# Three queues re-ordered in a gated conv/attention block on one Trainium2 core: weight sums, the first down chunk, and the last products

## The chip, the core and the metric

The kernel runs on one core of a Trainium2 chip. The metric is the device time of one execution in microseconds (us), taken as the median of several. A second source is one profiled execution, whose rows carry a start time, a duration, the engine and a line number (L326 is line 326). PE is TensorE, PEld its weight loads, DVE VectorE, ACT ScalarE, POOL GpSimd, SP SyncE; SPq, POOLq and ACTq rows are DMAs issued by those engines.

## What is computed

The reference is one layer of a streaming encoder over 512 positions and 1024 channels, in float32:

```
h = rms_norm(x)
[conv B | conv C | conv in | q | k | v | forget | gates] = h @ w_in
y_A = (B * dwconv3(C * xin)) @ w_out_conv ;  y_B = forgetting_attention(q, k, v) @ w_out_attn
x = x + (sigmoid(g_A) * y_A + sigmoid(g_B) * y_B) @ w_o
[a | b] = dwconv3(rms_norm(x) @ w_up)
x = x + (silu(a) * b) @ w_down
out = rms_norm(x)
```

`w_up` has 2 x 2816 columns, which are 44 blocks of 128, called up0 to up43 (block 2j is a, block 2j+1 is b of pair j, and j runs from 0 to 21). `w_down` has 2816 rows.

## The kernel before, in words

**Three products for one.** Activations stand transposed: 128 partitions of channels, 512 columns of positions. Each float32 factor is split into a high part in a shorter format and the rest (`hi`, `lo`), and a product is three TensorE passes, wh*xh, wl*xh and wh*xl (`mm3`, L300, and `passes`, L314). So each chunk of weights that is loaded is also split (`split`, L252): ScalarE copies it to `wh` (L274), VectorE subtracts to get `wl` (L278). Both have two buffers, so a chunk can be split while the one before it is in use. `passes` takes all products with wh first and those with wl after them, so `wl` may come later than `wh`. A whole up block takes TensorE 5.44 us; its first two of eight row blocks go through `passes`, which uses wl after eight matmuls.

**Seven products for eight.** Part of the gates (j from 3 to 7), up pairs 1, 2 and 5 (`SUP`), and most of the down projection are computed in pairs of 2x2 blocks with seven block products (`seven`, L786). Their weights come in two chunks for each step, P (plain blocks) and F (sums of blocks). The sums are made by DMAs between DRAM tensors `f` (`make_forms`, L190): six operations for each group of steps, alternately a copy issued by SP (`put`) and an adding DMA issued by POOL (`add`): f0 = x0, f0 += x1, f1 = f0, f1 += x1, f2 = f1, f2 += x2. Each waits for the one before it to land. They stand in a list with a slot number, and each call of `slot()` (L217) issues those that are due.

**The gate loop** (L947 to L979) runs over eight output blocks j. In each: `slot()` (L949), the two gate blocks, then the chunk mix j, then two products yc and ya with a `slot()` in front of each (L967), then the gating: two VectorE products (L975, L976), a POOL sum (L977), a ScalarE copy to `mh` (L978) and a VectorE subtraction to `ml` (L979). In j = 7 four loads of x are issued by POOL (L953) right after the first `slot()`. In this loop the list holds the sums for the up pairs 1, 2 and 5, three groups, with six operations each in slots 4k + g for operation k of group g: the copies f2 = f1 are in j = 5 (groups 0 and 1) and j = 6 (group 2), the last adds f2 += x2 are in j = 6 (group 0, third slot) and j = 7 (group 1 in the first slot, group 2 in the second).

**The order on an engine** is fixed before the launch by a planner: of the instructions that it reckons to be ready it takes the one that was written first. `keep` (L82) pins an instruction behind the one that was written just before it on the same engine, whatever that is. The DMAs of `slot()`, the loads of chunks and all matmuls are pinned. L953 and L977 are not.

**Evacuations put off.** `later` is a list of pieces of work with a price in us and a chunk from which they are due. `run_later` (L223), called by each `split`, issues pieces from the front of the list up to a budget (0.1 more is allowed), behind the two instructions of that split. Pieces that merge the seven-product up pairs (`merge`, L1150) carry a mark "e": z1 0.42, m1 0.7, u3 0.85, m2 0.7, fin0 0.7, tap0 1.4, fin1 0.7, tap1 1.4, and `glu`. While a marked piece is in the list, the budget is that of L285 (3.8 for an up chunk), and each further up block's evacuation is put on the list too, with the mark: a product with the norm factor (`mul`, 0.7, L1139), the causal filter (`taps`, 1.4: one ScalarE copy and two VectorE instructions, L561 to L565) and after the second block `glu`. Without a marked piece an evacuation is written at once, and the budget is 1.7 (L287). `glu` (L1195) multiplies silu(a) and b (POOL), and for each second pair adds six pieces that form and split the sums for the down projection (t13 and t24 at 0.85, four splits at 0.7; L1220 to L1233), due two to four chunks later, or four to six after the last pair of a phase, whose product goes to VectorE and is due three chunks later. If an older pair has such pieces left, `glu` first issues them all.

**Two phases.** Pairs 0 to 11 go through up and then the down projection (12 steps, P16 and F16 to P27 and F27), then pairs 12 to 21 and 8 steps (from P28). Between the up loop and the down projection all marked pieces are issued (L1311); `seven` then splits its first chunk unless that is done (`chunk`, L289). `split_next` (L780) splits the next chunk of the stream if it isn't split yet.

**The end.** The last two output blocks of the down projection are plain products in two halves of the columns; `fin_out` (L1376) then multiplies all eight blocks of a half with the norm factor, which TensorE has put into a PSUM bank `pb`, and stores them by five DMAs, from SP and ACT in turn. ScalarE copies the factor to `rs` in SBUF, since POOL does one of the five products and VectorE four.

Of the kernel before, what the change touches and what calls it, by code (L numbers as in the profile page):

```python
# [8 lines left out]
F32 = mybir.dt.float32  # L9
F32R = mybir.dt.float32r  # L10
AF = mybir.ActivationFunctionType
ALU = mybir.AluOpType

P = 128
D = 1024
S = 512
# [26 lines left out]
PHASES = ((0, 12), (12, NP))  # L43
# [27 lines left out]
def block_kernel(ctx, tc, xT, vecs, wv, win, wmix, wo, wup, wst, wdp, outT):  # L71
# [3 lines left out]
    nc = tc.nc  # L75
# [83 lines left out]
    def after_split():  # L159

        st = ExitStack()
        for ins in order.values():
            st.enter_context(tc.issue_after(ins))
        return st
# [4 lines left out]
    def load(upto):  # L169
        for k in range(len(raws), min(upto, len(stream) - 1) + 1):  # L170
            nm, src, ncol = stream[k]
            tag = tag_of(k)
            if held[tag] == NRAW[tag] or tag not in pools:
                return
            held[tag] += 1
            raw = pools[tag].tile([P, D], F32, tag=tag, name=f"raw_{nm}", bufs=NRAW[tag])
            if k == 0:

                keep(nc.scalar.dma_start(raw[:, VB:ncol], src[:, VB:]))
                keep(nc.sync.dma_start(raw[:, :VB], src[:, :VB]))  # L180
            else:
                keep(nc.sync.dma_start(raw[:, :ncol], src if tag == "raw" else made[src]))
            raws.append(raw[:, :ncol])
# [33 lines left out]
    def slot():  # L217

        while todo_bg and todo_bg[0][0] <= make_forms.slot:
            todo_bg.pop(0)[1]()  # L220
        make_forms.slot += 1

    def run_later(k, us):  # L223

        n = 0
        while n < len(later):
            if later[n][0] <= k and later[n][1] <= us + 0.1:
                us -= later[n][1]
                with after_split():
                    later.pop(n)[3]()  # L230
            elif later[n][0] <= k:
                return
            else:
                n += 1
# [17 lines left out]
    def split(hl=None):  # L252

        k = len(parts)
        if k == len(stream):
            return
        nm, _, ncol = stream[k]
        load(k + (LOOK if len(raws) > KB else AHEAD))
        if hl is None:
            hl = []  # L260
            for x in "hl":
                if k == 0:
                    wp.tile([P, PADW[x]], F32, tag=f"pad{x}", name=f"pad_{x}")
                w0 = VOFF if k < KB else 0
                hl.append(wp.tile([P, D], F32R, tag=f"w{x}", name=f"w{x}_{nm}", bufs=2)[:, w0 : w0 + ncol])
        hi, lo = hl
        raw = raws[k]
        if k == 0:
            for cs in (slice(VB, S + H), slice(0, VB)):
                keep(nc.vector.tensor_copy(hi[:, cs], raw[:, cs]))  # L270
        elif k == 1:
            keep(nc.vector.tensor_copy(hi, raw))
        else:
            ins = nc.scalar.activation(hi, raw, AF.Copy)  # L274
            order["hi"] = ins.ins
            if k < KB:
                keep(ins)
        ins = nc.vector.tensor_sub(lo, raw, hi.bitcast(F32))  # L278
        order["lo"] = ins.ins
        if k < KB:  # L280
            keep(ins)
        held[tag_of(k)] -= 1
        parts.append((hi, lo))
        if any(("e",) in w[2] for w in later):
            run_later(k, {"u": 3.8, "P": 1.6, "F": 1.2}[nm[0]])  # L285
            return
        run_later(k, {"u": 1.7, "P": 1.6, "F": 0.75, "i": 3.0, "m": 3.0, "d": 0 if nm == "dp1" else 2.1}.get(nm[0], 3.5))  # L287

# [123 lines left out]
    pb = [pb_[t // 2][:, (t % 2) * 4 * HD : (t % 2 + 1) * 4 * HD] for t in range(NT)]  # L412
# [333 lines left out]
    for idx in late:  # L746
        kind, i = divmod(idx, 4)
# [32 lines left out]
    def split_next():  # L780
        if len(parts) == chunk.n and stream[chunk.n][0] not in ("dp1", "dp2"):
            split()
# [104 lines left out]
    k = [c[0] for c in stream].index("mix1")  # L887
    for q in (0, 2):
        f, g = x_sums(slice(q, q + 2))
# [56 lines left out]
    make_forms(len(GATES), N0, "up")  # L946
    for j in range(KB):  # L947
        gs = []
        slot()  # L949
        if j == KB - 1:  # L950
            x1 = xp.tile([P, KB, S], F32, tag="x1", name="x1")
            for q in range(4):
                nc.gpsimd.dma_start(x1[:, 2 * q : 2 * q + 2, :], xT[:, 2 * q : 2 * q + 2, :])  # L953
        if j == 0:
            evac_gate(0, gs)(gp[0])
            evac_gate(8, gs)(gp[1])
        elif j < GJ:
            run_all(proj(20 + j, f"ga{j}", evac_gate(j, gs), acc))
            run_all(proj(28 + j, f"gb{j}", evac_gate(8 + j, gs), acc))
        else:  # L960
            if j == GJ:
                acc = ring(2, 7, 3, 4)
            seven(GATES[2 * (j - GJ) : 2 * (j - GJ) + 2], 2 * (j - GJ), {j: (0, 1, 5, 6)}, gate_form, done=gate_pair(j, gs))
        wh, wl = chunk(f"mix{j}")
        yc, ya = acc(f"yc{j}"), acc(f"ya{j}")
        for pp, hh, ll, o in ((yc, ych, ycl, 0), (ya, oth, otl, 4)):
            slot()  # L967
            for k in range(4):
                ks = slice((o + k) * P, (o + k + 1) * P)
                mm3(pp, wh[:, ks], wl[:, ks], hh[:, k, :], ll[:, k, :], k == 0, k == 3)  # L970
        if j >= GJ:
            split_next()
            flush()
        a, b = gs
        nc.vector.tensor_mul(a, a, yc)  # L975
        nc.vector.tensor_mul(b, b, ya)  # L976
        nc.gpsimd.tensor_add(a, a, b)  # L977
        nc.scalar.activation(mh[:, j, :], a, AF.Copy)  # L978
        nc.vector.tensor_sub(ml[:, j, :], a, mh.bitcast(F32)[:, j, :])  # L979
# [44 lines left out]
    def block(name, xh, xl, lead=False):  # L1024
        wh, wl = chunk(name)
        q = acc(f"p_{name}")
        for kb in range(KB):
            ks = slice(kb * P, (kb + 1) * P)
            if lead and kb < 2:
                if kb:  # L1030
                    passes([
                        (q[:, cs], 0, wh[:, b], wl[:, b], xh[:, a, cs], xl[:, a, cs], True, False)
                        for a, b in enumerate((slice(0, P), ks)) for cs in halves
                    ], 4)
                continue
            mm3(q, wh[:, ks], wl[:, ks], xh[:, kb, :], xl[:, kb, :], kb == 0, kb == KB - 1)
        return q
# [53 lines left out]
    fp = ctx.enter_context(tc.tile_pool(name="fp", bufs=1))  # L1091
# [22 lines left out]
    def up(j, ph, rb2, pu=None):  # L1114
        uu = []

        def tap(i, z):
            u = fp.tile([P, S], F32, tag="fu", name=f"fu{j}{i}", bufs=3)
            taps(u, z, CF + 3 * (2 * j + i))
            uu.append(u)  # L1120

        if j in SUP:
            c = len(GATES) + 2 * SUP.index(j)
            slot()
            seven(
                UPD[c - len(GATES) :][:2], c, {j: USETS[j]}, up_form, of="x",
                done=lambda i, banks, ids: merge(ph, j, banks, ids, rb2, tap, uu),
            )
            slot()
            return  # L1130
        evacs = []
        for i in range(2):
            slot()
            p = pu[i] if pu else block(f"up{2 * j + i}", x1h, x1l, True)
            z = [None]

            def mul(i=i, p=p, z=z):
                z[0] = fp.tile([P, S], F32, tag="fz", name=f"fz{j}{i}", bufs=4)
                nc.vector.tensor_mul(z[0], p, rb2)  # L1139

            evac = [(0.7, mul), (1.4, lambda i=i, z=z: tap(i, z[0]))]
            if i:
                evac.append((0, lambda: glu(ph, j, uu)))
            if any(("e",) in w[2] for w in later):
                later.extend((0, us, (("e",), acc.last) if x == 0 else (("e",),), f) for x, (us, f) in enumerate(evac))
            else:
                for _, f in evac:
                    f()
# [227 lines left out]
    def fin_out(t, rc):  # L1376
        hs = halves[t]
        pb = rstd_bc(rc, 2, (1, 5)[t], f"n3{t}")[:, : S // 2]
        rs = fp.tile([P, S], F32, tag="fu", name=f"rs{t}", bufs=3)[:, : S // 2]
        nc.scalar.activation(rs, pb, AF.Copy)  # L1380
        for g, (a, b) in enumerate(((0, 1), (1, 3), (6, 8), (3, 5), (5, 6))):
            y = x1[:, a:b, hs]
            eng, r = (nc.gpsimd, rs) if g == 2 else (nc.vector, pb)
            eng.tensor_mul(y, y, r.unsqueeze(1).to_broadcast([P, b - a, S // 2]))  # L1384
            keep((nc.sync, nc.scalar)[g % 2].dma_start(outT[:, a:b, hs], y))

    def warm_on(n):
# [121 lines left out]
```

## Time and profile before

| what | us |
|---|---|
| median of 3 runs (lowest to highest) | 697.87 (697.65 to 698.26) |
| the profiled execution, its own time | 698.61 |
| its span from first to last instruction | 696.8 |
| PE busy in the span | 686.7 |
| DVE, ACT, POOL busy | 530.9, 359.7, 180.7 |

The span is 1.8 us shorter than the time of its execution, and that execution is 0.74 us above the median. A row's bracket, as in "[1.55 <-ACT wh_P L274]", is the idle time of its engine just before it and the instruction that ended it. In a row with x6, six instructions in a row are merged. Matmuls overlap one another, so a matmul's duration (0.28 us) is longer than the step from one to the next (0.113 us).

### The profile page before, as it was taken

Reading aid. Unit: us, or ns where it says so; the run is one execution under the profiler, and the core shown is the slowest. Engines: PE = TensorE matmul, PEld = TensorE weight load, DVE = VectorE, ACT = ScalarE, POOL = GpSimd, SP = SyncE. Lnnn points to the kernel's source line nnn. Section 1 sums busy time; section 2 is a strip of 40 time slices with the busy share of each in tenths; the row PEclk is TensorE's granted clock in tenths of the full one; section 3 lists DMA queues with packets and bytes.
Section 4 is the critical chain, followed back from the end, with each engine's and each line's share of the span. In section 5 each row is a group of like instructions: output and inputs, shape, how many; then the busy total and the mean of one; then the engine's idle time right before and its main releaser. Section 6 shows DMA issues by size and latency. Waiting matters only on the chain.

```text
span 696.8 us, 14636 instructions
## 1 busy us (share of the span) xinstructions
PE 686.7 (99%) x5972; PEld 684.9 (98%) x5972; DVE 530.9 (76%) x824; ACT 359.7 (52%) x567; POOL 180.7 (26%) x196
## 2 busy tenths in 40 slices
PE   9999999999999999999999999999999999999996
PEld 9999999999999998999999999999999999999995
DVE  6677877776678776868869799988674677878793
ACT  5665655645565443446554455465443344445572
POOL 4134847532211201113523143210000313221001
PEclk9999999999999999999999999999999999999998
DMA  7528978542688687666799775536646686676513
GB/s 253 161 70 276 205 183 201 121 91 89 234 237 257 183 234 208 202 216 141 110 316 296 199 184 130 153 124 193 198 129 228 143 192 162 184 170 175 156 31 121
DMA packets 58387, 124.68 MB, mean 179 GB/s; under 512 B 5280, under 2 KB 26800, under 8 KB 58320
## 3 DMA queue, kind: packets, MB, share of 16 engines
q1 hardware_dynamic: 40776, 99.68, 44.0%
q0 software_dynamic: 16304, 22.88, 20.6%
q10 hardware_dynamic: 1240, 1.19, 0.5%
q8 instruction: 47, 0.77, 0.4%
q14 instruction: 20, 0.16, 0.1%
HBM read 121.57 MB, written 39.32 MB: 231 GB/s over the span
## 4 chain that ended last, share of the span: by engine, by line
PE 58%; DVE 2%; DMA 0%; ACT 0%; issue 0%; DVEq 0%; ACTq 0%
PE p_up L308 21%; PE dn L326 19%; PE p_up L326 7%; PE p_wo L308 6%; PE pdB L308 1%; PE pdA L308 1%; PE ya L308 1%; PE yc L308 1%; DMA raw_dp<-in_wdp_dram 0%; PE pc_n L343 0%; DVE fu L562 0%; DVE fu L565 0%; PE pb_n L362 0%; DVE gl L1231 0%; DVE wl_up L278 0%; DVE x L1384 0%
## 5 line engine op out<-in xcount | busy, mean ns | idle before, releaser
L308 PE MATMUL p_up<-x1h,wh_up 128*128 128x256 f32 x464 | 90.5, 276 | 0.0
L308 PE MATMUL p_up<-x1l,wh_up 128*128 128x256 f32 x464 | 90.3, 276 | 0.0
L308 PE MATMUL p_up<-x1h,wl_up 128*128 128x256 f32 x464 | 90.3, 276 | 0.0
L210 POOL DMA_DIRECT2D f<-in_wst_dram x57 | 66.1, 1311 | 15.6 <-DMA f<-f 15.3
L308 PEld LDWEIGHTS p_up<-x1h,wh_up 128*128 128x128 f32 x464 | 69.9, 188 | 0.0
L308 PEld LDWEIGHTS p_up<-x1l,wh_up 128*128 128x128 f32 x464 | 69.9, 188 | 0.0
L308 PEld LDWEIGHTS p_up<-x1h,wl_up 128*128 128x128 f32 x464 | 69.8, 188 | 0.0
L274 ACT ACTIVATE wh_up<-raw_up 128x1024 fp32r<-128x1024 f32 x38 | 40.2, 1058 | 55.8 <-PE p_up L308 46.2
L278 DVE TENSOR_TENSOR wl_F<-raw_F,wh_F 128x1024 fp32r<-128x1024 f32 (+1 forms) x36 | 46.9, 1304 | 17.8 <-ACT wh_F L274 17.8
L278 DVE TENSOR_TENSOR wl_up<-raw_up,wh_up 128x1024 fp32r<-128x1024 f32 x38 | 48.3, 1270 | 12.8 <-ACT wh_up L274 12.7
L308 PE MATMUL p_in<-xgh,wh_in 128*128 128x256 f32 x288 | 56.8, 279 | 0.0
L308 PE MATMUL p_in<-xgh,wl_in 128*128 128x256 f32 x288 | 56.6, 278 | 0.0
L308 PE MATMUL p_in<-xgl,wh_in 128*128 128x256 f32 x288 | 56.5, 278 | 0.0
L274 ACT ACTIVATE wh_F<-raw_F 128x1024 fp32r<-128x1024 f32 (+1 forms) x36 | 37.9, 1052 | 34.1 <-PE dn L326 26.6
L1204 POOL TENSOR_TENSOR ge<-fu,fu 128x512 f32<-128x512 f32 x11 | 17.6, 1602 | 138.6 <-DVE fu L565 119.1
L274 ACT ACTIVATE wh_P<-raw_P 128x768 fp32r<-128x768 f32 (+1 forms) x36 | 30.0, 834 | 31.4 <-PE dn L326 22.6
L308 PEld LDWEIGHTS p_in<-xgh,wh_in 128*128 128x128 f32 x288 | 44.7, 188 | 0.7
L326 PE MATMUL dn<-gh,wh_F 128*128 128x256 f32 x192 | 45.1, 276 | 0.0
L326 PE MATMUL dn<-gl,wh_F 128*128 128x256 f32 x192 | 45.1, 276 | 0.0
L278 DVE TENSOR_TENSOR wl_P<-raw_P,wh_P 128x768 fp32r<-128x768 f32 (+1 forms) x36 | 34.5, 958 | 13.6 <-ACT wh_P L274 9.0
L308 PEld LDWEIGHTS p_in<-xgl,wh_in 128*128 128x128 f32 x288 | 43.7, 188 | 0.0
L308 PEld LDWEIGHTS p_in<-xgh,wl_in 128*128 128x128 f32 x288 | 43.6, 188 | 0.0
(351 smaller groups left out, 2154.8 us busy)
## 6 DMA issues: line engine op xcount, KB each, us to landing
raw_up<-in_wup_dram SPq DMA_DIRECT2D x38, 512.0 KB, 3.9
raw_F<-f SPq DMA_DIRECT2D x35, 512.0 KB, 4.9
raw_P<-in_wst_dram SPq DMA_DIRECT2D x35, 384.0 KB, 4.7
raw_in<-in_win_dram SPq DMA_DIRECT2D x26, 512.0 KB, 3.5
f<-in_wst_dram POOLq DMA_DIRECT2D x35, 256.0 KB, 6.4
f<-in_wst_dram SPq DMA_DIRECT2D x17, 512.0 KB, 5.5
f<-in_wst_dram POOLq DMA_DIRECT2D x17, 512.0 KB, 8.1
f<-f SPq DMA_DIRECT2D x34, 256.0 KB, 5.6
```

Source lines behind the costliest of these rows:

```text
L210: return lambda: keep(nc.gpsimd.dma_start(dst, src, accum_op=ALU.add))
L274: ins = nc.scalar.activation(hi, raw, AF.Copy)
L278: ins = nc.vector.tensor_sub(lo, raw, hi.bitcast(F32))
L308: keep(nc.tensor.matmul(out[:, cs], w, x[:, cs], start=start and i == 0 and c == 0, stop=stop and i == 2 and c == len(cut) - 1,))
L326: keep(nc.tensor.matmul(out, wl if x == 1 else wh, xl if x == 2 else xh, start=opens and bk not in seen, stop=closes and bk not in left,))
L1204: keep(nc.gpsimd.tensor_mul(ge, a.rearrange(halves_of, h=2), b.rearrange(halves_of, h=2)))
```

## The change

Four edits. The budget for an up chunk while marked pieces wait goes from 3.8 to 4.2. In the gate loop the three `slot()` calls of an output block are made in line at its top, ahead of the gate blocks and of the loads of x in j = 7. After the last up block of each phase the next chunk (the first P chunk of the down projection) is split before that block's evacuation is written. In `fin_out` ScalarE's copy of the factor and POOL's product go; VectorE does all five products from PSUM, and the blocks are grouped anew with the same sizes in the same order of queues.

```diff
@@ split @@
         if any(("e",) in w[2] for w in later):
-            run_later(k, {"u": 3.8, "P": 1.6, "F": 1.2}[nm[0]])
+            run_later(k, {"u": 4.2, "P": 1.6, "F": 1.2}[nm[0]])
             return
@@ gate loop @@
     for j in range(KB):
         gs = []
-        slot()
+        for _ in range(3):
+            slot()
         if j == KB - 1:
             x1 = xp.tile([P, KB, S], F32, tag="x1", name="x1")
...
         for pp, hh, ll, o in ((yc, ych, ycl, 0), (ya, oth, otl, 4)):
-            slot()
             for k in range(4):
@@ up @@
             p = pu[i] if pu else block(f"up{2 * j + i}", x1h, x1l, True)
+            if i and j + 1 == PHASES[ph][1]:
+                split_next()
             z = [None]
@@ fin_out @@
         pb = rstd_bc(rc, 2, (1, 5)[t], f"n3{t}")[:, : S // 2]
-        rs = fp.tile([P, S], F32, tag="fu", name=f"rs{t}", bufs=3)[:, : S // 2]
-        nc.scalar.activation(rs, pb, AF.Copy)
-        for g, (a, b) in enumerate(((0, 1), (1, 3), (6, 8), (3, 5), (5, 6))):
+        for g, (a, b) in enumerate(((0, 1), (1, 3), (3, 5), (5, 7), (7, 8))):
             y = x1[:, a:b, hs]
-            eng, r = (nc.gpsimd, rs) if g == 2 else (nc.vector, pb)
-            eng.tensor_mul(y, y, r.unsqueeze(1).to_broadcast([P, b - a, S // 2]))
+            nc.vector.tensor_mul(y, y, pb.unsqueeze(1).to_broadcast([P, b - a, S // 2]))
             keep((nc.sync, nc.scalar)[g % 2].dma_start(outT[:, a:b, hs], y))
```

## The prediction, made before the changed kernel was run

> **What bounds the kernel now.** I read the page's busy times first, then the TensorE timeline for its gaps, then the other engines' timelines around each gap, and the stretches at the end.
>
> ```profile
> PE 686.7 (99%) x5972; PEld 684.9 (98%) x5972; DVE 530.9 (76%) x824; ACT 359.7 (52%) x567; POOL 180.7 (26%) x196
> 271.65 0.38 PE L326 MATMUL dn<-xgh,wh_P 128*128 128x256 f32 x1 [1.55 <-ACT wh_P L274]
> 471.32 0.97 PE L326 MATMUL dn<-gh,wl_P 128*128 128x256 f32 x6 [0.78 <-DVE wl_P L278]
> 690.28 0.38 ACT L1380 ACTIVATE rs<-pb_n 128x256 f32<-128x256 f32 x1 [1.06 <-PE pb_n L362]
> 690.70 1.95 DVE L1384 TENSOR_TENSOR x<-x,pb_n 128x256 f32<-128x256 f32 x4 [1.28 <-ACT rs L1380]
> 690.74 1.27 POOL L1384 TENSOR_TENSOR x<-x,rs 128x512 f32<-128x512 f32 x1 [4.82 <-ACT rs L1380]
> ```
>
> TensorE is busy for 686.7 of 696.8 us and the change takes no product from it. So the change can gain only where TensorE stands still: at 270 (1.55), at 470 (0.78) and in the tail after TensorE's last product. It can lose wherever a weight split comes late, for most of the kernel runs without a gap.
>
> **Part 1: the slots of the gate loop.** What is the gap at 270?
>
> ```profile
> 215.56 2.16 POOL L953 DMA_DIRECT2D x<-in_xT_dram  x4 [7.75 <-DVE xtl L883]
> 251.25 1.30 POOL L977 TENSOR_TENSOR ga<-ga,gb 128x512 f32<-128x512 f32 x1 [10.43 <-DVE gb L976]
> 259.44 0.61 SPq L207 DMA_DIRECT2D f<-f  x1
> 265.45 0.69 DVE L976 TENSOR_TENSOR gb<-gb,ya 128x512 f32<-128x512 f32 x1
> 267.84 1.04 POOL L210 DMA_DIRECT2D f<-in_wst_dram  x1 [15.29 <-DMA f<-f]
> 268.44 1.76 POOL L977 TENSOR_TENSOR ga<-ga,gb 128x512 f32<-128x512 f32 x1
> 270.24 0.63 ACT L978 ACTIVATE mh<-ga 128x512 fp32r<-128x512 f32 x1 [3.75 <-POOL ga L977]
> 270.77 0.83 ACT L274 ACTIVATE wh_P<-raw_P 128x768 fp32r<-128x768 f32 x1
> 244.86 0.38 ACT L914 ACTIVATE gz<-dn 128x256 f32<-128x256 f32 x1
> 259.82 0.38 ACT L914 ACTIVATE gz<-dn 128x256 f32<-128x256 f32 x1
> 276.62 0.38 ACT L914 ACTIVATE gz<-dn 128x256 f32<-128x256 f32 x1
> ```
>
> The sum L977 of j = 5 had its operands at 266.14 (265.45 + 0.69) and began at 268.44, because an add stood ahead of it in POOL's queue, waiting for a copy that was issued at 259.44 and landed at 267.84. ScalarE's `mh` waited for the sum, the split of the next P chunk stood behind `mh`, and TensorE waited for that. This add is written in j = 6 or 7, behind L977 of j = 5. Only one of the last three could be ahead of it: the add of group 2, whose pin is to the instruction written before it, L953, and those loads ran at 215.56. So the planner was free to move it. With three slots in line it is pinned to the add of group 1, and that to L977 of j = 6. The sum then starts at 266.2, `mh` is written by 268.2, wh_P by about 269, and TensorE gets to that chunk at 270.1 (271.65 less 1.55) without a wait. The same point of the loop comes after 14.96 us (244.86 to 259.82) and here after 16.80, so what the stall cost is **-1.84**.
>
> What the edit adds: copies move ahead of loads in SP's queue. In j = 5 two copies go from behind the loads of j = 5 to behind the load of 243.93, and SP waits there for their adds.
>
> ```profile
> 237.59 3.24 POOL L210 DMA_DIRECT2D f<-in_wst_dram  x3
> 243.93 0.33 SPq L182 DMA_DIRECT2D raw_P<-in_wst_dram  x1
> 253.66 0.33 SPq L182 DMA_DIRECT2D raw_F<-f  x1
> DMA to landing us min/median/max: 3.1/5.6/14.5
> ```
>
> The second of the adds is issued by 238.7. At the longest landing of any such DMA, 14.5, that is 253.2, and SP's next load is at 253.66, when its buffer comes free. So 0; a rise needs a landing that this trace doesn't have. In j = 2 and 3 copies move the same way, past loads whose chunks are used a whole output block later. POOL's adds keep their neighbours but for that one.
>
> **Part 2: the first down chunk and the budget.** The gap at 470 waits for wl_P16.
>
> ```profile
> 463.77 0.85 ACT L274 ACTIVATE wh_P<-raw_P 128x768 fp32r<-128x768 f32 x1 [0.18 <-PE p_up L308]
> 469.12 1.28 DVE L1231 TENSOR_TENSOR gl<-go,gh 128x512 fp32r<-128x512 f32 x2
> 470.32 0.95 DVE L278 TENSOR_TENSOR wl_P<-raw_P,wh_P 128x768 fp32r<-128x768 f32 x1
> 469.02 0.28 PE L326 MATMUL dn<-gh,wh_P 128*128 128x256 f32 x1
> 631.67 0.96 DVE L278 TENSOR_TENSOR wl_P<-raw_P,wh_P 128x768 fp32r<-128x768 f32 x1 [0.19 <-ACT wh_P L274]
> 636.03 0.28 PE L326 MATMUL dn<-gh,wh_P 128*128 128x256 f32 x1
> ```
>
> Its wh was there at 464.62, but VectorE ran other work until 470.32. Going through the list by hand shows why: in phase 0 each up block adds 2.1 of evacuation and, each second block, 4.5 of sums, so 4.35 a block against a budget of 3.8. Marked pieces never run out, and the last ones (up22, up23, `glu` 11, the six pieces of pair 4) are all issued at once, ahead of P16. With 4.2 the list runs out at the split of up18; from there evacuations are written at once, as in phase 1, where the split of the first P chunk was done at 632.63, 3.4 us before TensorE began that chunk at 636.03. TensorE began that chunk of phase 0 at 469.02, stopped at 470.38 (its twelve matmuls with wh at 0.113, the step in the merged row of 420.96 below: (0.62 - 0.28) / 3) and went on at 471.32: **-0.94**. The early `split_next` alone would help less, as pair 4's sums t13 and t24 and the four splits are older still. In phase 1 it moves pair 10's pieces by one chunk; by the budgets they are still issued ahead of step P31, the first that uses them. I take 0.
>
> The bigger budget has a price. At the split of up14 the old list issues u3, m2, fin0 and tap0 of pair 5; the new one has done u3 and m2 before, and issues fin0, tap0, fin1, tap1 and, through `glu`, all six pieces of pair 1, which the old list issues one split later. All these are written ahead of the split of up15.
>
> ```profile
> 411.04 1.21 DVE L278 TENSOR_TENSOR wl_up<-raw_up,wh_up 128x1024 fp32r<-128x1024 f32 x1
> 414.90 0.75 DVE L562 SCALAR_TENSOR_TENSOR fu<-ua,vec,fu 128x511 f32<-128x511 f32 x1 [0.79 <-ACT fu L561]
> 416.36 1.22 DVE L278 TENSOR_TENSOR wl_up<-raw_up,wh_up 128x1024 fp32r<-128x1024 f32 x1
> 417.49 0.68 DVE L1182 SCALAR_TENSOR_TENSOR ub<-ub,rb_n 128x512 f32<-128x512 f32 x1
> 421.09 1.89 DVE L1231 TENSOR_TENSOR gl<-go,gh 128x512 fp32r<-128x512 f32 x3
> 422.90 0.69 DVE L1139 TENSOR_TENSOR fz<-p_up,rb_n 128x512 f32<-128x512 f32 x1
> 423.15 1.29 POOL L1211 TENSOR_TENSOR go<-fu,fu 128x512 f32<-128x512 f32 x1 [7.67 <-DVE gl L1231]
> 423.50 2.03 DVE L278 TENSOR_TENSOR wl_up<-raw_up,wh_up 128x1024 fp32r<-128x1024 f32 x1
> 420.96 0.62 PE L326 MATMUL p_up<-x1h,wl_up 128*128 128x256 f32 x4
> ```
>
> Before, VectorE had wl_up15 at 416.36 and finished pair 1's pieces at 422.90. After, from 411.04 on, it has the same work without wl_up15 in the middle (417.49 - 416.36 = 1.13) and without the idle 0.79, which other pieces now fill: 422.90 - 411.04 - 1.13 - 0.79 = 9.94, so wl_up15 starts at 420.98 and ends at 422.20. TensorE wants it at 420.96. That is a wait of **+1.2**. It is nothing if the planner finds a moment with no older piece ready and puts the split in. At 464.62 to 470.32 it found none in a list of the same kind. If POOL's product takes the split's place as at 423.50, it is 2.03 - 1.22 = 0.81 more. I take 1.2, with 0 and 2.0 for the range: the split follows directly on VectorE's last piece, and POOL's product waits for that piece too.
>
> The Trainium skill bears on that (SBUF — State Buffer, "Who interferes with whom"): a VectorE instruction with two SBUF inputs and a GpSimd one that reads SBUF exclude each other, and the one that comes second waits for the whole of the other. The rows of 423.15 and 423.50 agree: the split took 2.03 beside a product that began first, 1.22 alone. By that rule the wait would be 2.0 if POOL's product begins first here, and 1.2 if not.
>
> After this wait VectorE is 1.2 us less behind TensorE. I went on through up16 to up18 with the same durations: by my count of pieces each wl comes 0.5 to 2 us ahead of its use, so nothing more.
>
> **Part 3: the tail.** VectorE's products began when ScalarE's copy was over (690.70 against 690.28 + 0.38), though they read `pb`, which ScalarE had from 690.28 on. Without the copy they can start at about 690.28: 0.42 earlier. VectorE then does five. A product of two blocks takes 0.60 in a row of them (1.95 = 0.60 + 0.60 + 0.33 + 0.42 for two of two blocks and two of one), so five end at 690.28 + 1.95 + 0.60 = 692.83 in place of 692.65: 0.18 later. Which of the two decides?
>
> ```profile
> 692.00:693.00 1.00, 0.00 (x0) 0.00 (x0) 0.65 (x2) 0.00 (x0) 0.01 (x1) 0.59 0.69 236
> 693.00:694.00 1.00, 0.00 (x0) 0.00 (x0) 0.00 (x0) 0.00 (x0) 0.00 (x0) 0.50 1.09 383
> 694.00:695.00 1.00, 0.00 (x0) 0.00 (x0) 0.00 (x0) 0.00 (x0) 0.00 (x0) 0.50 1.09 382
> 695.00:696.80 1.80, 0.00 (x0) 0.00 (x0) 0.00 (x0) 0.00 (x0) 0.00 (x0) 0.50 0.07 24
> ```
>
> The last column is GB/s. From 693 to 695 the stores run at 383 GB/s, so they are bound by their bytes: what counts is when the stream starts, not when the last product ends. The second store becomes ready 0.42 earlier and the others follow at 0.60 for 256 KB, faster than 383 GB/s drains them (0.68). So **-0.4**; the range is -0.5 to +0.2.
>
> The Trainium skill has a rule on this wait (PSUM — Partial Sum Buffer, "PSUM bank collisions raise a hardware error"): two engines may not use one PSUM bank at a time, not even both to read, so that an order must be put between them. The row at 690.70 agrees; by the rule the 0.42 goes with the copy, and without it the sum would be +0.2 here.
>
> **Sum.** -1.84 - 0.94 + 1.2 - 0.4 = -1.98 against the profiled execution's 698.61. That one is 0.74 above the median, of which no gap named here is a part, so I take it from the median: 697.87 - 1.98 = **695.9**.
>
> **Rivals.** *No wait at up15*: the planner puts the split in earlier. For it: a single idle moment in the planner's reckoning is enough. Against: 470.32. 697.87 - 1.84 - 0.94 - 0.4 = 694.7. *The add isn't held back*: something else lets POOL's queue stall, or the freed time meets another wait in the gate loop. For it: I infer the add's identity from its place. Against: L953's early start and the count of adds. 697.87 - 0.94 + 1.2 - 0.4 = 697.7. *Slower*: the bigger budget keeps VectorE's wl behind for several blocks. Its place is up15 to up18; with POOL's product in front each wait is up to 2.0, and three of them are 6.0, which gives 697.87 - 3.18 + 6.0 = 700.7. It decides from 3.2 us of such waits on. For it: the rows above leave VectorE no idle time between 414.90 and 425.53. Against: each wait of TensorE gives VectorE as much time back.
>
> **How the numbers follow.** Forecast 0.50, no wait 0.24, the add 0.17, slower 0.09. The range reaches from 694.3 (no wait, and the tail at its best) to 697.5 (the forecast with 2.0 at up15 and +0.2 in the tail is 697.3). A measurement of this kernel can tell about 0.2%, 1.4 us, from no change: faster than 696.47 are nearly all of the first two, within are the third and a few of the first, so 0.73, 0.18 and 0.09.
>
> **What would show it.** Right: no add ahead of L977 of j = 5 and no gap at 270; no gap at the first P chunk of phase 0, with wl_P done some us ahead; a TensorE gap of about 1.2 at the eighth matmul of up15, ended by VectorE's wl_up; no rs, products from about 0.1 after `pb`. Wrong: gaps at up16 to up18 or at P31, a copy on SP that holds back a load, or stores that end later than now.

## The result, and the profile after

The changed kernel takes **695.98 us** (median of 8 runs, 695.72 to 696.46). The kernel before, run beside it, took 698.36 (8 runs; its first three, which the prediction knew, had a median of 697.87). The ratio is 0.9967, 95% interval 0.9956 to 0.9978: faster by 2.4 us, 1.5 to 3.1 by the interval. The profiled execution took 695.75 with a span of 693.9, against 698.61 and 696.8.

First the page's busy times of the changed kernel, then its table of TensorE's waits (us in total, times, longest).

```profile
PE 686.2 (99%) x5972; PEld 684.6 (99%) x5972; DVE 531.4 (77%) x826; ACT 359.2 (52%) x565; POOL 178.3 (26%) x194
```

```profile
PE warm L115 <- DVE ones L107: 1.1, 1, 1.1
PE p_up L326 <- DVE wl_up L278: 0.6, 1, 0.6
```

TensorE has the same 5972 instructions. Both waits of before, for `wh_P` and for `wl_P`, are gone, and one is new: the wait for an up chunk that the prediction had put at up15. Behind the start, no other is left. (Lines from `up` to `fin_out` are numbered two higher than before.)

The gate loop at 270, by the timelines of VectorE, POOL and ScalarE of the changed kernel (start, us, engine, line, operation):

```profile
259.72 0.38 ACT L914 ACTIVATE gz<-dn 128x256 f32<-128x256 f32 x1
...
265.35 0.69 DVE L976 TENSOR_TENSOR gb<-gb,ya 128x512 f32<-128x512 f32 x1
266.12 1.29 POOL L977 TENSOR_TENSOR ga<-ga,gb 128x512 f32<-128x512 f32 x1 [13.66 <-DVE gb L976]
267.35 1.04 POOL L210 DMA_DIRECT2D f<-in_wst_dram  x1
267.44 0.63 ACT L978 ACTIVATE mh<-ga 128x512 fp32r<-128x512 f32 x1 [1.04 <-POOL ga L977]
267.98 0.83 ACT L274 ACTIVATE wh_P<-raw_P 128x768 fp32r<-128x768 f32 x1
...
274.68 0.38 ACT L914 ACTIVATE gz<-dn 128x256 f32<-128x256 f32 x1
...
282.32 2.09 POOL L210 DMA_DIRECT2D f<-in_wst_dram  x2
```

and two rows of POOL's timeline of the kernel before:

```profile
269.68 1.52 POOL L210 DMA_DIRECT2D f<-in_wst_dram  x1
...
284.26 1.03 POOL L210 DMA_DIRECT2D f<-in_wst_dram  x1
```

No add stands ahead of the sum L977 any more. The one right behind it (267.35) is that of group 0, which is written there and stood there before too (269.68). The one that had been ahead of it is now behind the next sum, where two run (282.32) and one had run before (284.26). The sum starts 0.08 after its last operand is written (265.35 + 0.69) where it had started 2.3 late, `mh` and `wh_P` follow at once, and the step between the two gate copies is 274.68 - 259.72 = 14.96 in place of 16.80.

The blocks up14 to P16, by the timelines of TensorE, VectorE and POOL of the changed kernel:

```profile
403.00 1.29 POOL L1213 TENSOR_TENSOR go<-fu,fu 128x512 f32<-128x512 f32 x1 [18.43 <-ACT fu L561]
403.35 1.50 DVE L562 SCALAR_TENSOR_TENSOR fu<-fz,vec,fu 128x511 f32<-128x511 f32 x1
...
410.08 1.21 DVE L278 TENSOR_TENSOR wl_up<-raw_up,wh_up 128x1024 fp32r<-128x1024 f32 x1
...
418.11 0.28 PE L326 MATMUL p_up<-x1h,wh_up 128*128 128x256 f32 x1
...
418.54 1.22 DVE L278 TENSOR_TENSOR wl_up<-raw_up,wh_up 128x1024 fp32r<-128x1024 f32 x1
418.77 2.15 POOL L1213 TENSOR_TENSOR go<-fu,fu 128x512 f32<-128x512 f32 x1 [8.02 <-DVE gl L1233]
...
419.81 0.74 PE L326 MATMUL p_up<-x1h,wl_up 128*128 128x256 f32 x4 [0.63 <-DVE wl_up L278]
...
464.66 1.45 DVE L278 TENSOR_TENSOR wl_P<-raw_P,wh_P 128x768 fp32r<-128x768 f32 x1
...
467.99 0.28 PE L326 MATMUL dn<-gh,wh_P 128*128 128x256 f32 x1
...
469.35 0.84 PE L326 MATMUL dn<-gh,wl_P 128*128 128x256 f32 x6
...
633.91 0.28 PE L326 MATMUL dn<-gh,wh_P 128*128 128x256 f32 x1
```

TensorE begins up15 at 418.11, wants the low half eight products later and gets it at 419.81. P16's low half is written by 466.11, 1.9 us before TensorE begins that chunk. To price both stalls I use landmarks rather than the idle in the brackets. They are fixed points of the program, here the first product of up15, of P16, and of P28 (the first down chunk of phase 1), and the time from one to the next. Four rows of the kernel before's timelines that were not shown yet, POOL's last L1211 ahead of these blocks (L1213 at 403.00 above) and the tap of VectorE beside it, up15's first product, and the product that makes the factor `pb`:

```profile
404.95 2.11 POOL L1211 TENSOR_TENSOR go<-fu,fu 128x512 f32<-128x512 f32 x1 [18.43 <-ACT fu L561]
405.83 1.78 DVE L562 SCALAR_TENSOR_TENSOR fu<-fz,vec,fu 128x511 f32<-128x511 f32 x1
...
420.06 0.28 PE L326 MATMUL p_up<-x1h,wh_up 128*128 128x256 f32 x1
...
689.57 0.61 PE L362 MATMUL pb_n<-ident,rc_n 128*128 128x128 f32 x4
```

From up15 to P16 it was 469.02 - 420.06 = 48.96 and is 49.88: the new stall costs **0.92**. From P16 to P28 it was 167.01 and is 165.92: the old one had cost **1.09**. The edits for blocks up0 to P16 together are worth only 0.17 by these two profiles.

The tail, by the timelines of TensorE and VectorE and by stretches (the last column is GB/s):

```profile
687.26 0.61 PE L362 MATMUL pb_n<-ident,rc_n 128*128 128x128 f32 x4
...
687.91 2.54 DVE L1383 TENSOR_TENSOR x<-x,pb_n 128x256 f32<-128x256 f32 x5 [0.80 <-PE pb_n L362]
```

```profile
690.10:691.10 1.00, 0.00 (x0) 0.00 (x0) 0.35 (x2) 0.00 (x0) 0.00 (x0) 1.00 1.08 383
691.10:692.10 1.00, 0.00 (x0) 0.00 (x0) 0.00 (x0) 0.00 (x0) 0.00 (x0) 0.66 1.10 384
692.10:693.90 1.80, 0.00 (x0) 0.00 (x0) 0.00 (x0) 0.00 (x0) 0.00 (x0) 0.50 0.11 38
```

The products start 0.65 after the factor's product in place of 1.13, the stores run at the same 383 GB/s, and from that product to the end of the span it takes 6.64 in place of 7.23. So the span's -2.9 is -1.84, -0.17 and -0.59, and -0.3 in two stretches in which kernels differ as much without any edit there: 0.10 ahead of the gate loop's last step, where profiles of kernels that are the same up to there differ by up to 0.6 (259.72 to 260.32), and 0.19 between P28 and the factor, where all fourteen profiles lie between 53.35 and 53.56.

### The profile page after: what moved, and what is told of

It is laid out like the page before. It is cut to its first block, busy times and chain, and to the rows that moved or that the text cites. A ratio compares the mean times of both kernels' runs of the same rounds, so it can differ in the third digit from the quotient of the medians.

```text
span 693.9 us, 14635 instructions
## 1 busy us (share of the span) xinstructions
PE 686.2 (99%) x5972; PEld 684.6 (99%) x5972; DVE 531.4 (77%) x826; ACT 359.2 (52%) x565; POOL 178.3 (26%) x194
## 4 chain that ended last, share of the span: by engine, by line
PE 96%; DVE 3%; issue 0%; ACT 0%; DVEq 0%
PE dn L326 24%; PE p_up L308 21%; PE p_in L308 14%; PE p_up L326 6%; PE p_wo L308 6%; PE yc L308 3%; PE ya L308 3%; PE pa L472 2%; PE pb L474 2%; PE p_q L308 2%; PE p_k L308 2%; PE p_gb L308 2%; PE p_ga L308 2%; PE o L653 2%; PE tp L636 1%; PE pdB L308 1%
```

## The experiments

All runs in one table. The steps are those above, in us, from one profile each: the gate step on ScalarE, up15 to P16, P16 to P28, and the factor's product to the end (the span is given to 0.1). Ratios are to the kernel before on the same chip; the first row's median is that of the changed kernel's chip.

| kernel | gate | up15-P16 | P16-P28 | tail | median | ratio, 95% interval |
|---|---|---|---|---|---|---|
| before | 16.80 | 48.96 | 167.01 | 7.23 | 698.36 | |
| changed | 14.96 | 49.88 | 165.92 | 6.64 | 695.98 | 0.9967, 0.9956 to 0.9978 |
| e1_slots | 14.96 | 48.96 | 167.00 | 7.23 | 696.81 | 0.9980, 0.9970 to 0.9990 |
| e2_loads | 14.96 | 48.96 | 166.99 | 7.33 | 696.73 | 0.9982, 0.9973 to 0.9992 |
| e3_old_budget | 14.96 | 48.95 | 167.18 | 6.63 | 696.21 | 0.9978, 0.9969 to 0.9987 |
| e4_no_early_split | 14.96 | 49.90 | 165.92 | 6.59 | 695.99 | 0.9967, 0.9953 to 0.9981 |
| e5_tail_only | 16.77 | 48.96 | 167.20 | 6.67 | 697.50 | 0.9992, 0.9979 to 1.0004 |
| e6_copy_back | 14.96 | 49.96 | 165.92 | 7.05 | 696.47 | 0.9976, 0.9967 to 0.9986 |
| e7_late_budget | 14.96 | 52.55 | 165.92 | 6.66 | 698.79 | 1.0009, 1.0000 to 1.0017 |
| e8_budget_only | 16.58 | 49.95 | 165.92 | 7.28 | 697.94 | 0.9994, 0.9982 to 1.0005 |
| e9_middle_budget | 14.96 | 49.86 | 167.62 | 6.64 | 697.37 | 0.9991, 0.9982 to 1.0000 |
| e10_from_up19 | 14.96 | 48.96 | 167.63 | 6.65 | 696.63 | 0.9982, 0.9973 to 0.9991 |
| e11_pair5_later | 14.96 | 48.96 | 167.52 | 6.64 | 696.98 | 0.9983, 0.9974 to 0.9992 |
| e12_after_again | 14.96 | 49.88 | 165.92 | 6.64 | 695.91 | 0.9969, 0.9959 to 0.9980 |

Medians of the kernel before lay between 697.83 and 698.36 from one chip to another. The steps repeat to 0.2 wherever an edit doesn't touch them, mostly to 0.1, so I go by the steps where less than 1 us is at stake.

### Part 1: what frees the stall at 270

**e1: the slots alone**, on the kernel before.

```diff
-        slot()
+        for _ in range(3):
+            slot()
...
-            slot()
```

> The kernel before with the three slots in line and nothing else. My theory (an add of the weight sums stands ahead of the sum of j = 5 on POOL and holds it back until its copy has landed): the stall of 1.55 at 270 goes, the step from the gate copy of j = 6 to that of j = 7 on ScalarE falls from 16.80 to 14.96, the stalls at 470 (0.78) and before the last stores stay as before, no stall comes at the eighth matmul of up15, and the span is 1.84 shorter (694.9 to 695.1). Rival (what goes at 270 comes back later, because VectorE and SP run on by their own schedule): the stall goes at 270, but the products of the first down chunk or the norm's sum start less than 1 us earlier than before.

The gate step is 14.96, and what was gained there stays: P16 begins at 467.05 (469.02 before), P28 at 634.05, the factor's product is at 687.47, 2.10 earlier. The rival falls. (The median is 1.2 below that of the kernel before on this chip, 0.7 to 2.1 by the interval, which holds the 1.84 of the step.)

**e2: the pin alone.** Slots as before, the loads of x written behind them (behind the products yc and ya of j = 7).

```diff
-        if j == KB - 1:
-            x1 = xp.tile([P, KB, S], F32, tag="x1", name="x1")
-            for q in range(4):
-                nc.gpsimd.dma_start(x1[:, 2 * q : 2 * q + 2, :], xT[:, 2 * q : 2 * q + 2, :])
...
+        if j == KB - 1:
+            x1 = xp.tile([P, KB, S], F32, tag="x1", name="x1")
+            for q in range(4):
+                nc.gpsimd.dma_start(x1[:, 2 * q : 2 * q + 2, :], xT[:, 2 * q : 2 * q + 2, :])
```

> The kernel before with its slots where they were, but the four loads of x written at the end of j = 7 in place of its start, so that the add of group 2 in j = 7 is no longer pinned to them alone. My theory (it is the add of group 2 of j = 7, pinned to the loads that ran at 215.56, which was free to move ahead of the sum of j = 5): pinned to the add before it, it can't move, the stall at 270 goes without a change of the slots, and the span is 1.84 shorter (694.9 to 695.1). Rival (what helps is that copies go out earlier on SP, with the slots in line): the copies are as late as before, the stall at 270 stays, and the span is within 0.3 of before (696.5 to 697.1).

The timelines of SP and POOL of e2, where the add had stood ahead of the sum:

```profile
259.43 0.47 SPq L207 DMA_DIRECT2D f<-f  x1
266.29 1.29 POOL L977 TENSOR_TENSOR ga<-ga,gb 128x512 f32<-128x512 f32 x1 [13.66 <-DVE gb L976]
267.52 1.04 POOL L210 DMA_DIRECT2D f<-in_wst_dram  x1
...
282.49 2.08 POOL L210 DMA_DIRECT2D f<-in_wst_dram  x2
```

The order of sums and adds is that of the changed kernel here too, and the step is 14.96, without any slot moved. The copy goes out as late as before (259.43, and 259.44 before). So the add was free to move because what stood before it in the order were the loads of x, which had long run; and the slots help by giving it another neighbour, not by sending copies out earlier.

### Part 2: which edit does what between up15 and F16

**e8: the budget alone**, on the kernel before (3.8 to 4.2).

> The kernel before with the budget of 4.2 and nothing else. My theory: the stall at 470 goes (0.8 to 1.1 less), a stall of 0.6 to 1.2 comes at the eighth matmul of up15, the stall at 270 (1.55) stays, and the span is within 0.4 of before (696.4 to 697.2). Rival (the wait at up15 comes only with the slots in line, which bring TensorE there earlier while VectorE runs behind): no stall at up15, and the span is 0.8 to 1.1 shorter.

TensorE's timeline has the stall at 270 as before, and up15's:

```profile
271.42 0.39 PE L326 MATMUL dn<-xgh,wh_P 128*128 128x256 f32 x1 [1.34 <-ACT wh_P L274]
...
421.52 0.74 PE L326 MATMUL p_up<-x1h,wl_up 128*128 128x256 f32 x4 [0.63 <-DVE wl_up L278]
```

The budget makes the stall at up15 (49.95) and removes that at P16 (165.92) by itself. The rival falls. The two nearly cancel: from up15 to P28 the five profiles with 4.2 throughout (changed, e4, e6, e8, e12) take 215.80 to 215.88, the four with the budget and the order of before (before, e1, e2, e5) 215.95 to 216.16. This part gains 0.1 to 0.4, and nearly all of the kernel's gain is that of the slots and the tail.

**e4: the changed kernel without the early split.**

```diff
-            if i and j + 1 == PHASES[ph][1]:
-                split_next()
```

> The changed kernel without the early split. My theory (with the budget of 4.2 the list has run out long before P16, so the early split adds nothing): the split of P16 on VectorE ends more than 1 us before TensorE needs its low part at about 469.3, no stall there, the stall at up15 as in the changed kernel (0.4 to 0.8), and the span within 0.3 of it (693.6 to 694.2). Rival (the early split is what removes the stall at 470): the stall is back with 0.6 to 1.0, and the span is 0.6 to 1.0 longer (694.5 to 694.9).

All its steps are those of the changed kernel to 0.05, and so is the median. With 4.2 the early split does nothing.

**e3: the early split without the budget** (3.8).

> The changed kernel with the old budget of 3.8 and the early split kept. The prediction's sentence (the early split would help less, as pair 4's sums and the four splits are older still): the stall at the first products with the low part of P16 stays at 0.5 to 0.9, the stall of about 0.6 at up15 goes, and the span is within 0.4 of the changed kernel. Rival, by the order in which the list hands out its pieces: the split of P16 is written ahead of the products of up22 and up23, glu 11 and most of pair 4, so the stall at P16 goes as well, and the span is 0.6 to 0.9 below the changed kernel (693.0 to 693.3), unless what is now written behind P16 makes the next split (F16) late by 0.3.

The timelines of VectorE and TensorE of e3:

```profile
462.79 0.96 DVE L278 TENSOR_TENSOR wl_P<-raw_P,wh_P 128x768 fp32r<-128x768 f32 x1
463.66 1.51 DVE L1223 TENSOR_TENSOR go<-ge 128x256 f32<-128x256 f32 x1
...
470.76 1.21 DVE L278 TENSOR_TENSOR wl_F<-raw_F,wh_F 128x1024 fp32r<-128x1024 f32 x1
...
472.03 1.21 PE L326 MATMUL dn<-gh,wl_F 128*128 128x256 f32 x8 [0.87 <-DVE wl_F L278]
```

The split of P16 runs ahead of all of pair 4's sums (L1223 on), so the stall at 470 is gone, and up15 has none: the prediction's sentence falls. The rival is right in the order, and its reservation decides, three times as large as I allowed: what now stands behind P16 makes F16's low half late by 0.87 in the row. The step from P16 to P28 is 167.18, even a little above before's 167.01: the early split alone moves the stall by one chunk.

So each budget pays once, at up15 (0.92 with 4.2) or at F16 (1.26 over the undisturbed 165.92 with 3.8). I tried four ways of paying neither.

**e7: 3.8 up to up14, 4.2 from up15 on.**

```diff
-            run_later(k, {"u": 4.2, ...
+            run_later(k, {"u": 3.8 if nm[0] == "u" and int(nm[2:]) < 15 else 4.2, ...
```

> The changed kernel with the old budget of 3.8 up to up14 and 4.2 from up15 on. My theory (the stall at up15 is made by the pieces that the bigger budget puts ahead of the split of up15): this stall (0.63 in the trace of the changed kernel, about 0.8 in all) goes, the split of P16 is still done ahead of its use, and the span is 0.6 to 0.9 below that of the changed kernel (693.0 to 693.3). Rival (the work that isn't done before up15 is only pushed on, and makes a later split late): a stall of 0.3 or more at up16 to up23 or at P16, and the span within 0.3 of the changed kernel.

The timelines of VectorE (splits of up17 and up18) and TensorE of e7:

```profile
427.56 1.22 DVE L278 TENSOR_TENSOR wl_up<-raw_up,wh_up 128x1024 fp32r<-128x1024 f32 x1
...
436.47 1.21 DVE L278 TENSOR_TENSOR wl_up<-raw_up,wh_up 128x1024 fp32r<-128x1024 f32 x1
...
437.74 0.73 PE L326 MATMUL p_up<-x1h,wl_up 128*128 128x256 f32 x4 [2.15 <-DVE wl_up L278]
...
449.76 0.74 PE L326 MATMUL p_up<-x1h,wl_up 128*128 128x256 f32 x4 [0.78 <-DVE wl_up L278]
```

The stall at up15 is gone and two larger ones come, 2.15 at up18 and 0.78 at up20: 8.9 us pass between two splits that TensorE wants 5.4 apart. My theory falls and the rival is right. Between them the full timeline has two taps, a product of an evacuation and all six pieces of pair 2: pair 1's pieces no longer stand ahead of up15, but what is caught up, pair 2's pieces among it, now stands ahead of up18.

**e9: a budget of 4.0. e10: 3.8 through up18, 4.4 from up19 on.**

> The changed kernel with a budget of 4.0, between the old and the new. Going through the list by hand: the six pieces of pair 1 stay behind the split of up15, as with 3.8, and of what 3.8 leaves behind the split of P16 the sums t13 and t24 of pair 4 and the product of up22 are done before it, some 1.9 of VectorE's work. My theory (each stall is the work that the list puts ahead of one split): no stall at up15, none at P16, the stall of 0.87 at F16 gone or under 0.2, and a span 0.7 to 1.0 below the changed kernel's 693.9 (692.9 to 693.2). Rival (work that is put off comes back ahead of another split, as with 3.8 up to up14): a stall of 0.3 or more somewhere from up16 to F16, and a span of 693.4 or more.

> The changed kernel with the old budget of 3.8 through up18 and 4.4 from up19 on. By the list: no pieces of pair 1 ahead of up15, and the list is empty at the split of up22, so that only two pieces of pair 4 and four that P16 needs anyway are left at P16. My theory: no stall at up15, P16 or F16, and a span 0.7 to 1.0 below the changed kernel's 693.9 (692.9 to 693.2). Rival (catching up puts too much ahead of a split, here that of up22, behind the products of up20 and up21 and their evacuation): a stall of 0.5 or more at up20 to up23, and a span of 693.4 or more.

TensorE's timeline, e9 and then e10:

```profile
446.87 0.73 PE L326 MATMUL p_up<-x1h,wl_up 128*128 128x256 f32 x4 [0.30 <-DVE wl_up L278]
...
471.37 0.38 PE L326 MATMUL dn<-gh,wh_F 128*128 128x256 f32 x1 [1.24 <-ACT wh_F L274]
```

```profile
471.06 0.38 PE L326 MATMUL dn<-gh,wh_F 128*128 128x256 f32 x1 [1.26 <-ACT wh_F L274]
```

Neither has a stall at up15. e9 has one at up20, which is 0.30 in its row and 0.90 by the step from up15 to P16 (49.86 in place of 48.96), and both stall at F16 by more than e3 (167.62 and 167.63 against 167.18). What ends the wait is now not VectorE's low half but ScalarE's high half. e10 does what I wanted in up15 to P16 (48.96) and loses 1.71 behind it. The rival of e9 is right; that of e10 is right in sign and not in place.

**e11: e3 with the last pair begun later.** If pair 4's four last splits were what F16 waits for, they have to go behind it; the buffer that pair 5 takes over from pair 4 had forced them ahead.

```diff
+        inner = j + 1 < PHASES[ph][1] or ph
+
+        def rest():
+            flush_only([("q", x) for x in range(q)])
+            go = fp.tile([P, 6, 2 * P], F32, tag="gr", name=f"go{q}")
...
+        if inner:
+            rest()
         else:
...
+            later.append((k + 3, 0.7, (("q", q),), rest))
```

> The changed kernel with the old budget of 3.8, the early split kept, and the last pair of phase 0 (pair 5) begun three chunks later: what must be written before it, the last four splits of pair 4, no longer has to stand ahead of the split of F16. My theory (the stall of 0.87 at F16 with 3.8 was made by these four, some 2.1 of VectorE's and ScalarE's time): no stall at up15, none at P16, none over 0.2 at F16, the step from the first product of P16 to the first of P28 back at 165.9 (167.18 with 3.8 alone), and a span of 692.9 to 693.2. Rival (pair 5 then comes too late for P20, the first chunk that uses it): a stall of 0.5 or more at P20 or behind it, and a span of 693.5 or more.

The timelines of VectorE, ScalarE and TensorE of e11, and then ScalarE's of the changed kernel at the same place:

```profile
468.56 0.75 DVE L565 SCALAR_TENSOR_TENSOR fu<-fz,vec,fu 128x510 f32<-128x510 f32 x1
...
469.40 0.63 ACT L1201 ACTIVATE fu<-fu 128x512 f32<-128x512 f32 x1 [1.66 <-DVE fu L565]
469.94 1.04 ACT L274 ACTIVATE wh_F<-raw_F 128x1024 fp32r<-128x1024 f32 x1
...
471.03 0.38 PE L326 MATMUL dn<-gh,wh_F 128*128 128x256 f32 x1 [1.14 <-ACT wh_F L274]
```

```profile
467.65 0.63 ACT L1201 ACTIVATE fu<-fu 128x512 f32<-128x512 f32 x1 [2.15 <-DVE fu L565]
468.19 1.06 ACT L274 ACTIVATE wh_F<-raw_F 128x1024 fp32r<-128x1024 f32 x1
```

My theory falls again. The four splits are behind F16 now, and the stall stays (167.52, and 1.14 in the row). The high half of F16 stands on ScalarE behind the Silu of up22 (L1201), which waits for VectorE's tap of up22 (L565, over at 469.31). In the changed kernel the same Silu runs at 467.65, 0.34 before TensorE begins P16, and in e11 1.72 behind it (469.40, P16 at 467.68): VectorE took the product of up22, which the tap needs, at 464.06 there, and in e11 at 466.30, behind the sums of pair 4 (both in the full timelines). The rival, a stall at P20, didn't come either. Whether there is an order with neither stall stays open. Of the versions tried none is ahead of the changed kernel. Its step from up15 to P28, 215.80, is the shortest of all (before 215.97, e3 216.13, e11 216.48, e10 216.59, e9 217.48, e7 218.47).

**e12: the changed kernel once more**, beside e11.

> The changed kernel once more, beside the version with the later pair 5 on the same chip: a median of 695.7 to 696.4 and the one stall of 0.63 at up15, so that a difference of 0.9 between the two can be told from a difference between chips.

695.91 and 0.63: as expected, and e11 is 1.1 behind it on the same chip.

### Part 3: the tail

**e5: the new last products alone**, on the kernel before.

```diff
-        rs = fp.tile([P, S], F32, tag="fu", name=f"rs{t}", bufs=3)[:, : S // 2]
-        nc.scalar.activation(rs, pb, AF.Copy)
-        for g, (a, b) in enumerate(((0, 1), (1, 3), (6, 8), (3, 5), (5, 6))):
+        for g, (a, b) in enumerate(((0, 1), (1, 3), (3, 5), (5, 7), (7, 8))):
...
```

> The kernel before with the new last products alone (no copy on ScalarE, five products on VectorE). My theory (the products waited for the copy, and from then on the stores are bound by their bytes): from the start of ScalarE's or VectorE's first read of the factor to the end of the span 0.4 to 0.6 less than before, the stalls at 270 (1.55) and 470 (0.78) as before, and the span 0.4 to 0.6 shorter (696.2 to 696.4). Rival (the end is set by the last product, which comes 0.18 later): the span is 0.1 to 0.2 longer.

The tail is 6.67 in place of 7.23, so the rival falls. The span, 696.8, isn't shorter: this execution was 0.47 late before the gate loop's last step already (its copy at 260.29, 259.82 before). The time's interval holds both no gain and the 0.6.

**e6: the copy put back**, used by nothing.

```diff
+        rs = fp.tile([P, S], F32, tag="fu", name=f"rs{t}", bufs=3)[:, : S // 2]
+        nc.scalar.activation(rs, pb, AF.Copy)
```

> The changed kernel with ScalarE's copy of the factor put back, though nothing uses it: VectorE's five products read the factor itself. If the copy and the products can't read the factor at the same time: the products start when the copy is over, 0.4 later than without it, and from the factor to the end of the span it takes 0.3 to 0.5 longer than in the changed kernel (6.64). Rival (the products read beside the copy, and the gain came from POOL's product that is gone): the products start with the copy, and the tail is within 0.1 of 6.64.

The timelines of TensorE, ScalarE and VectorE of e6:

```profile
687.55 0.61 PE L362 MATMUL pb_n<-ident,rc_n 128*128 128x128 f32 x4
...
688.20 0.38 ACT L1382 ACTIVATE rs<-pb_n 128x256 f32<-128x256 f32 x1 [1.00 <-PE pb_n L362]
688.61 2.54 DVE L1385 TENSOR_TENSOR x<-x,pb_n 128x256 f32<-128x256 f32 x5 [1.22 <-ACT rs L1382]
```

The products use nothing of the copy, and still start when it is over, 1.06 after the factor's product in place of 0.65; the tail grows by 7.05 - 6.64 = 0.41. So 0.41 of the tail's 0.59 is the copy.

## Why the prediction was right, point by point

- **The whole.** 695.9 was said and 695.98 measured, with the forecast's case: all four named effects came, at their places. That the figure is so close is luck: two errors lie behind it that nearly cancel. The terms sum to -2.60 (-1.84, -1.09, +0.92, -0.59) where -1.98 was said, and the three runs of before had a median 0.5 below that of the eight beside the changed kernel. One sum is wrong: by its own terms the range's lower end is 697.87 - 1.84 - 0.94 - 0.5 = 694.6, not 694.3.
- **Part 1, -1.84: right, and measured -1.84.** The cause and the undisturbed step of 14.96 are what was forecast. That the size is exact holds for this profile of the kernel before: with the same gate loop the step was 16.77 in e5 and 16.58 in e8, so the stall cost 1.81 and 1.62 there. e1 shows that nothing takes the gain back later, e2 shows which add it was and why it could move. That the copies on SP hold back no load is right too: in the changed kernel SP issues the two of j = 5 from 244.21 on, has done so by 249.14, and issues its next load at 253.56 (253.66 before).
- **P16, -0.94: right cause, measured 1.09.** The forecast took the time up to the first product after the stall. The six products from there on took 0.97 in their row and take 0.84 undisturbed (469.35): 0.13 of the missing 0.15.
- **up15, +1.2: right place and cause, measured 0.92.** e3 and e10 hold pair 1's pieces behind that split and have no stall there. The stall is 0.80 up to the first product (419.81 - 419.01, eight steps of 0.113 behind 418.11) and 0.12 in the four from there (0.74 for the 0.62 of before). The step that was mis-sized is the start of `wl_up15`: said 420.98, which is 419.03 on the new kernel's clock (up15 begins 1.95 earlier), and it came at 418.54. Of these 0.49, 0.27 had come by the split of up14 (410.08, where the rows of before give 411.04 - 1.95 and 1.26 for the pieces u3 and m2 ahead of it, 410.35). From 402.77 before and 400.83 after, VectorE has the same instructions ahead of these pieces, and all that differs is one tap (L562) that met POOL's product: 1.78 at 405.83 before, 1.50 at 403.35 after. The two engines met differently (POOL's product took 2.11 and 1.29), which the forecast couldn't see. The other 0.22 is nearly all idle of VectorE that the new order fills. I had put it at 0.79, by the bracket at 414.90. The full timeline gives 0.99: that row begins 1.46 behind the one ahead of it where 0.60 is undisturbed, and the next (415.69) 0.79 behind it in place of 0.66. And VectorE's split at 418.54 began before POOL's product, so it took its 1.22 undisturbed: the 0.81 of the range's upper end did not come. Behind up15 no wait was forecast and none came; the low halves of up16 to up18 were written 3.3, 2.5 and 2.1 ahead of their use, where 0.5 to 2 was said.
- **"The early split_next alone would help less, as pair 4's sums t13 and t24 and the four splits are older still": wrong as put.** e3 shows the split of P16 ahead of all of pair 4. That it gains nothing is true for another reason: the wait goes to F16. With 4.2 it does nothing (e4), and the 0 taken for phase 1 holds: from P28 to the factor the changed kernel is no different from kernels without the edit.
- **The tail, -0.4: right, measured -0.59.** e6 gives the copy 0.41, against 0.42 in the forecast. The other 0.18, not much above the 0.1 to which the tails repeat, comes with VectorE's fifth product in place of POOL's and the other order of stores; I counted that as a cost that the stores hide, and by these profiles it was a gain. Which of the two makes it stays open.
- **Where two engines met.** POOL's product took 2.15 at 418.77 behind a split that had begun first, and 1.29 at 423.15 in the kernel before, where the split took the 2.03: the trace agrees in both directions with the Trainium skill on VectorE and GpSimd excluding each other (SBUF — State Buffer, "Who interferes with whom"). In e6 a copy that nothing uses cost 0.41, which agrees with the Trainium skill on two readers of one bank (PSUM — Partial Sum Buffer, "PSUM bank collisions raise a hardware error"). Whether the chip itself or only an order in the program made the products wait, the trace doesn't tell.

## What to carry to other kernels

Where VectorE has a backlog, a budget for put-off work doesn't make the backlog smaller: it chooses in front of which weight split it stands. Before changing it, list what would stand ahead of each split, on every engine that the split needs, and price it up to the point where the list has run out: of the five budgets tried here with the early split (3.8, 4.0, 4.2 and two mixed ones) only one came out below the kernel before's 215.97 from up15 to P28, and that by 0.17. And a DMA or an engine instruction ordered only behind something that is long done has, for a planner like this one, no order at all; give it a neighbour that runs when it should.

## What the runs showed that I had not expected

- A stall of TensorE costs more than the idle that its row shows: 1.55 in the row at 270 and 1.84 by the landmarks; 0.63 and 0.92 at up15; 0.78 and 1.09 at P16; 0.87 and 1.26 at F16 in e3; 0.30 and 0.90 at up20 in e9. At up15 the difference is all in rows: 0.17 because the idle is counted from the end of a product of 0.28 while products undisturbed start 0.11 apart, and 0.12 because the four products behind the stall take 0.74 and not 0.62.
- ScalarE, busy for only half of the span (52% in the changed kernel), was what TensorE waited for in e9, e10 and e11: a high half stood behind a Silu that waited for VectorE (469.94 and 469.40 in e11, where TensorE had left up23, whose buffer this high half takes over, by 468.1).
